# Two more slots for weight blocks in a decoder kernel, kept in mixer tiles that idle during the feed-forward blocks

## The chip, the cores and the metric

The kernel runs on one core of one Trainium2 chip. The core has a matrix engine (PE, with a queue of its own for weight loads, PEld), a vector engine (DVE), a scalar engine (ACT), a general engine (POOL) and a queue engine that issues transfers (SP). They run side by side and wait for each other by semaphores; each takes its instructions in order. The metric is device time in microseconds (us) for one execution of the whole program; the time of a kernel is the median of its runs.

## What is computed

Two layers of a decoder trunk on 256 tokens of width 1024, in float32. Each layer is a feed-forward block, a mixer and a second feed-forward block:

```python
h = x + 0.5 * (silu(n1(x) @ w_gate) * (n1(x) @ w_up)) @ w_down      # d_ff 2816
u = n(h);  P = u @ w_in                                             # one projection
h = h + concat(A(P), B(P), C(P)) @ w_out
y = h + 0.5 * (silu(n2(h) @ w_gate2) * (n2(h) @ w_up2)) @ w_down2
```

A is sparse attention with an indexer that chooses 64 keys per query (4 heads, one key head), B is attention over blocks of 256 (4 heads; with 256 tokens each query sees its own block alone), C is attention with forget gates (8 heads). A and B use rotary positions. All weights, about 195 MB with both layers, come from the chip's memory once per execution.

## The kernel before, in words

**Split products.** Every float32 weight block of 128 x 2048 (1 MB) is split into a high part `wh` (ACT, a cast, line 168) and a low part `wl` (DVE, a subtraction, line 172). PE multiplies high by high, high by low and low by high (`threes`, line 512; the matmul itself is line 366). There are four pairs of split buffers.

**Seven products instead of eight.** A feed-forward block works through 2816 columns in six units (`UNITS`, line 54). A unit of 512 columns has the weight quarters B11 and B21 (of w_gate, upper and lower half of the rows) and B12 and B22 (of w_up). The units marked "S" (1, 3 and 4) take seven products P1 to P7 of sums of quarters, after Strassen. For these, B12's tile is loaded from w_up, and then a second transfer, issued on POOL with addition (line 131, the "accumulate" below), adds B11 to it. P5 uses that sum. P6, P7 and P4 use sums that DVE forms in place (line 299, `pre`). P1, P2 and P3 use B11, B21 and B22 as they are.

**Slots.** `Weights` keeps a list of all weight blocks in the order of use (`raws`) and loads them in this order on SP (line 139). A load needs one of six tiles, the slots (`raw0` to `raw5`, 8 KB in each partition). A slot becomes free when its last reader has run, nearly always the subtraction of line 172, sometimes a `pre` of line 299. `issue` (line 110) is called at each release, and stops at the first block that finds no slot. From the first block of w_in on, the sixth slot is held back for two tiles of the mixer (`hold`, line 114), and given back at the end of the mixer's projections (`release_hold`, line 1216).

**Order of work.** The order of all products is written out by hand (`ffn_order`, line 59), and so is the mixer's (`at_step`). PE, ACT and DVE run their instructions in the order in which the program records them. `W.pump` puts a cast and a subtraction between the other instructions after each product; it looks two blocks ahead.

**The places that matter here.** Unit 1 of a block ends with P4 in PSUM bank A. Its Silu (ACT, line 653) reads that bank. Before the Silu, ACT's order has the cast of unit 3's P5 block (line 168) and the split of a transposed tile (line 680). After some transposes (line 676), PE's next product is P1 of unit 3, which starts bank A anew. In the mixer, C's queries and keys are kept in `cqa` and `cka`, all values in `va`, and A's mask in `amask`; these had tiles of their own for the whole program, and only the mixer uses them. C's queries and keys are transposed on PE in four steps (`c_T`, line 1247).

Of the kernel before, what the change touches and what calls it, by code (L numbers as in the profile page):

```python
# [18 lines left out]
P = 128  # L19
# [10 lines left out]
IDX_SCALE = (8 ** -0.5) * (64 ** -0.5)  # L30
RSQRT_MAGIC = 1597463007.0 - (1 << 22) - (1 << 30)

SLOTS = 6
SPLIT_BUFS = 4
LEAD = 2
OUT_TAIL = 3
# [37 lines left out]
class Weights:  # L74


    def __init__(self, tc, base, split_pool):
        self.nc = tc.nc
        self.base, self.split_pool = base, split_pool
        self.raws, self.pieces = [], []  # L80
        self.left = []
        self.raw_tiles, self.slot = {}, {}
        self.free = list(range(SLOTS))
        self.hold = False
        self.split_tiles, self.srcs = {}, {}
        self.n_dma = self.n_pre = self.n_high = self.n_low = self.n_used = self.n_done = 0
        self.held, self.adds = [], []
# [22 lines left out]
    def issue(self, limit=None):  # L110
        while self.n_dma < min(len(self.raws), limit or len(self.raws)):
            shape, parts, stage, more = self.raws[self.n_dma]
            if stage == "in":
                self.hold = True
            ok = [x for x in self.free if x < SLOTS - 1 or not self.hold]
            if not ok:
                return
            self.free.remove(ok[0])
            n = shape[0] * shape[1]
            t = self.base.tile([P, 2048], F32, name="raw", tag=f"raw{ok[0]}")  # L120
            self.slot[self.n_dma] = ok[0]
            self.raw_tiles[self.n_dma] = t[:, :n].rearrange("p (a b) -> p a b", a=shape[0])
            for i in range(len(parts)):
                self.load(self.n_dma, i)
            if more is not None:
                self.adds.append((self.raw_tiles[self.n_dma], more))
            self.n_dma += 1
# [2 lines left out]
        while self.adds:  # L130
            self.nc.gpsimd.dma_start(*self.adds.pop(0), accum_op=ALU.add)  # L131

    def release_hold(self):
        self.hold = False
        self.issue()

    def load(self, raw, i):
# [60 lines left out]
def kernel(ctx: ExitStack, tc: tile.TileContext, x, ffn1_norm, ffn1_w_gate, ffn1_w_up, ffn1_w_down,  # L198
# [63 lines left out]
    def add_ffn(wg, wu, wd):  # L262
        gsrc, usrc, dsrc = (w.rearrange("(k p) c -> p k c", p=P) for w in (wg, wu, wd))
        blocks, whole = {}, {}

        def block(i, kind):
            if (i, kind) not in blocks:
                _, f0, nf = UNITS[i]
                cols = slice(f0 * P, (f0 + nf) * P)
                if UNITS[i][0] == "H":  # L270
                    ks = slice(0, 4) if kind == "H0" else slice(4, 8)
                    parts = [(np.s_[:, :, 0:256], gsrc[:, ks, cols]), (np.s_[:, :, 256:512], usrc[:, ks, cols])]
                else:
                    src = gsrc if kind in ("B11", "B21") else usrc
                    k0 = 4 if kind in ("B21", "B22") else 0
                    parts = [(np.s_[:], src[:, k0:k0 + 4, cols])]
                more = gsrc[:, 0:4, cols] if UNITS[i][0] == "S" and kind == "B12" else None
                blocks[i, kind] = W.add_raw((4, 512), parts, "ffn", more)
            return blocks[i, kind]

        def raw(i, kind):
            return W.raw_tiles[blocks[i, kind]]

        def plain(i, kind, op=None):
            whole[i, op] = W.add_piece(lambda: raw(i, kind), [block(i, kind)], 2048, 4)

        def summed(i, op):
            if op == "P5":
                rids = [blocks[i, "B12"]]
                whole[i, op] = W.add_piece(lambda: raw(i, "B12"), rids, 2048, 4)  # L290
                return
            p, q, home, sign, prior = dict(P6=("B22", "B12", "B12", ALU.add, "P5"),
                                           P7=("B12", "B11", "B11", ALU.subtract, "P1"),
                                           P4=("B21", "B12", "B21", ALU.add, "P2"))[op]
            for r in (p, q):
                block(i, r)

            def pre():
                V.tensor_tensor(raw(i, home), raw(i, p), raw(i, q), op=sign)  # L299

            whole[i, op] = W.add_piece(lambda: raw(i, home), [block(i, home)], 2048, 4, pre,
                                       [blocks[i, r] for r in (p, q)], whole[i, prior])

        def down(f):
            r = W.add_raw((2, D), [(np.s_[:], dsrc[:, f:f + 2, :])], "ffn")
            W.add_piece(lambda: W.raw_tiles[r], [r], 2048, 2)

        for what in ffn_order():
            if what[0] == "G":
                if what[3] == 0:  # L310
                    plain(what[1], what[2])
            elif what[0] == "P":
                if what[2] in ("P1", "P2", "P3"):
                    if what[2] == "P1":
                        block(what[1], "B12")
                    plain(what[1], dict(P1="B11", P2="B21", P3="B22")[what[2]], what[2])
                else:
                    summed(what[1], what[2])
            elif what[0] == "d" and what[1] % 2 == 0:
                down(what[1])  # L320
        for f in TAIL[::2]:
            down(f)
# [31 lines left out]
    cs = cst[:, 384:640].rearrange("p (t c) -> p t c", t=2)  # L354
    causal = cp.tile([P, 3 * P], F32, name="causal")
    identr = cp.tile([P, P], F32R, name="identr")
    cqa = [at.tile([P, 8, 66], F32, name=f"cqa{t}", tag=f"cqa{t}") for t in range(2)]
    cka = [at.tile([P, 8, 66], F32, name=f"cka{t}", tag=f"cka{t}") for t in range(2)]
    va = [at.tile([P, 13, 65], F32, name=f"va{t}", tag=f"va{t}") for t in range(2)]
    for t in range(2):  # L360
        G.memset(cqa[t][:, :, 65:66], 1.0)
        G.memset(cka[t][:, :, 64:65], 1.0)
        G.memset(va[t][:, :, 64:65], 1.0)

    def mm(o, l, r, start, stop):
        T.matmul(o, l, r, start=start, stop=stop, skip_group_check=True)  # L366

# [381 lines left out]
    def mixer(l, entry, nxt):  # L749
# [83 lines left out]
            mm(o, q, k[1], False, stop)  # L833

        st = {}
        swapped = base.tile([P, 2, 512], F32, name="swapped", tag="sg")
        turns = itertools.count()

        def post_iq(ps):
            rot = base.tile([P, 2, 2, S], F32, name="iqr", tag="ov0")  # L840
            rot = [[rot[:, t, jj] for jj in range(2)] for t in range(2)]
            for t in range(2):
                for jj in range(2):
                    evac(rot[t][jj], ps[t][:, jj * S:(jj + 1) * S], t)
                    rope(heads(rot[t][jj], 4), cs[:, t, 0:64], cs[:, t, 64:128], V)
            qs = {}

            def split(jj):
                qs[jj] = [stack(rot[t][jj]) for t in range(2)]

            def turn_iq(jj):
                if jj == 0:
                    st["iqT"] = base.tile([P, 2, 4, S], F32R, name="iqT", tag=f"raw{SLOTS - 1}")
                queries_T(st["iqT"][:, jj], qs[jj])

            for jj in range(2):
                at_step(7 + jj, lambda jj=jj: split(jj))
                at_step(9 + jj, lambda jj=jj: turn_iq(jj))

        def post_ib(ps):  # L860
# [85 lines left out]
                                    imm_value=-3e38)  # L946

            def amask():
                am = at.tile([P, 3 * P], F32, name="amask", tag="amask")
                V.tensor_scalar(am[:, P:2 * P], st["score"][1][:, 0:P], -2e38, None, op0=ALU.is_gt)  # L950
                for t in range(2):
                    V.scalar_tensor_tensor(am[:, 2 * t * P:(2 * t + 1) * P], st["score"][t][:, t * P:(t + 1) * P],
                                           -2e38, future, op0=ALU.is_gt, op1=ALU.max)
                V.tensor_scalar(am, am, NEG, None, op0=ALU.mult)
                st["amask"] = am
# [53 lines left out]
        def post_b(ps):  # L1009
# [17 lines left out]
                    bk.append(twice.rearrange("p h s d -> p h (s d)"))  # L1027

            def bk_turn():
                st["bkT"] = base.tile([P, 2, 4, S], F32R, name="bkT", tag=f"raw{SLOTS - 1}")  # L1030
                keys_T(st["bkT"], bk)

            bk = []
# [179 lines left out]
        while side:  # L1213
            step[0] += 1
            run_side()
        W.release_hold()

        acc = [bank("acc") for _ in range(4)]

# [45 lines left out]
        for i in range(n + 1):  # L1265
            if i < n:
                scores(i)
            if i == n - 1:
                nxt = nxt()
            if i > 0:  # L1270
                flip(i - 1)
            if i < n:
                exps(i)
            if i in (3, 5, 7, 9):
                c_T((i - 3) // 2)
            if i not in (3, 5, 9, n):
                next(halves)
            if 0 < i < n:
                values(i - 1)
                if i > 2 and i % 2:  # L1280
                    outT((i - 3) // 2)
        for _ in halves:
            raise AssertionError
        return tail(acc, lhs, taken, OUT_ORDER[8 - OUT_TAIL:], 1.0, nxt,
                    (lambda: values(n - 1), lambda: outT(n // 2 - 1), lambda: None))


    def before_mixer(l):
# [73 lines left out]
```

## Time and profile before

| what | us |
|---|---|
| median of 3 runs | 1052.88 (1050.73 to 1057.02) |
| the profiled execution | 1049.79 |
| its span, first to last instruction | 1048.0 |
| PE busy | 1023.8 (98%) |
| DVE busy | 819.6 (78%) |
| ACT busy | 602.5 (57%) |
| POOL busy | 167.7 (16%) |
| bytes moved, and rate over the span | 196.74 MB, 188 GB/s |

A row of the timeline has the start in us, the duration, the engine, the line, the operation, output and inputs, and in brackets how long the engine stood before it and who ended that. Successive equal instructions stand in one row (x8) with the time from the first start to the last end. "SPq" rows are issues of transfers, not the transfers. A row of waits has who waited for whom, the total in us, how often, and the longest. A row of stretches has, for each engine, the busy time and the number of instructions, then the granted PE clock (1.00 is full), the busy share of the DMA engines and GB/s.

### The profile page before, as it was taken

How to read it: one execution, taken by the hardware profiler on the slowest of the kernel's cores; microseconds unless marked ns; L12 is line 12 of the kernel's file. 1: busy time of each engine (PE TensorE's matmuls, PEld its weight loads, DVE VectorE, ACT ScalarE, POOL GpSimd, SP SyncE). 2: the span in 40 equal slices, each digit the busy share in tenths (PEclk: the TensorE clock that was granted, in tenths of full speed). 3: DMA queues.
4: the chain of work that ended last, by engine and by line, in shares of the span. 5: the costliest groups of instructions: out<-in, count | busy, mean ns of one | idle time of the engine just before them, and what ended most of it. 6: DMA issues, size and time to landing. Idle time of an engine off the chain costs nothing. (4 is left out here: it accounts for less than half of the span.)

```text
span 1048.0 us, 12900 instructions
## 1 busy us (share of the span) xinstructions
PE 1023.8 (98%) x4982; PEld 857.2 (82%) x4982; DVE 819.6 (78%) x990; ACT 602.5 (57%) x687; POOL 167.7 (16%) x187
## 2 busy tenths in 40 slices
PE   9998999999999999999999999999999999999998
PEld 7887888897888788788878878888978878878887
DVE  5787969778777688786967878797797767779785
ACT  6554656478554656545664655556766546646461
POOL 1000040167610000000000000402766000000000
PEclk9999999999999999999999999999999999999999
DMA  9855866545362437493963749393445426284931
GB/s 351 255 168 174 282 193 246 164 167 164 139 220 92 114 137 229 163 296 115 351 194 118 247 155 302 109 327 121 166 163 168 165 88 199 82 280 136 306 121 41
DMA packets 94418, 196.74 MB, mean 188 GB/s; under 512 B 7314, under 2 KB 19986, under 8 KB 94356
## 3 DMA queue, kind: packets, MB, share of 16 engines
q1 hardware_dynamic: 87152, 180.64, 49.6%
q0 software_dynamic: 6336, 12.58, 6.6%
q10 hardware_dynamic: 868, 2.69, 0.7%
q8 instruction: 39, 0.64, 0.2%
q14 instruction: 23, 0.19, 0.1%
HBM read 194.85 MB, written 1.05 MB: 187 GB/s over the span
## 5 line engine op out<-in xcount | busy, mean ns | idle before, releaser
L172 DVE TENSOR_TENSOR wl<-raw,wh 128x2048 fp32r<-128x2048 f32 (+2 forms) x208 | 470.0, 2277 | 103.5 <-ACT wh L168 101.3
L168 ACT CAST wh<-raw 128x2048 fp32r<-128x2048 f32 (+2 forms) x208 | 389.8, 1892 | 124.3 <-PE ps_acc L366 46.1
L366 PE MATMUL ps_acc<-wh,hT 128*128 128x512 f32 (+1 forms) x704 | 185.9, 389 | 0.0
L366 PEld LDWEIGHTS ps_acc<-wh,hT 128*128 128x128 f32 x704 | 131.2, 188 | 26.8
L366 PE MATMUL ps_gu<-wh,x 128*128 128x512 f32 (+2 forms) x512 | 124.0, 385 | 0.0
L366 PE MATMUL ps_acc<-wl,hT 128*128 128x512 f32 (+1 forms) x352 | 105.9, 388 | 0.0
L366 PEld LDWEIGHTS ps_gu<-wh,x 128*128 128x128 f32 x512 | 92.8, 192 | 14.1
L131 POOL DMA_DIRECT2D raw<-in_ffn_w_gate_dram x12 | 15.9, 1322 | 490.6 <-DMA raw<-in_ffn_w_up_dram 275.4
L299 DVE TENSOR_TENSOR raw<-raw 128x2048 f32<-128x2048 f32 x36 | 82.4, 2288 | 0.1
L366 PEld LDWEIGHTS ps_acc<-wl,hT 128*128 128x128 f32 x352 | 65.9, 188 | 13.6
L366 PE MATMUL ps_A<-wh,A 128*128 128x512 f32 x256 | 65.6, 398 | 8.9 <-ACT tmp L653 8.9
L366 PE MATMUL ps_C<-wh,A 128*128 128x512 f32 x256 | 65.4, 395 | 0.1
L366 PE MATMUL ps_gu<-wl,x 128*128 128x512 f32 (+2 forms) x256 | 64.6, 374 | 0.0
L366 PE MATMUL ps_B<-wh,A 128*128 128x512 f32 x256 | 63.7, 391 | 0.0
L366 PEld LDWEIGHTS ps_A<-wh,A 128*128 128x128 f32 x256 | 46.6, 188 | 18.8 <-ACT tmp L653 9.9
L366 PEld LDWEIGHTS ps_C<-wh,A 128*128 128x128 f32 x256 | 47.6, 189 | 10.1 <-issue 0.4
L366 PEld LDWEIGHTS ps_B<-wh,A 128*128 128x128 f32 x256 | 47.8, 188 | 9.8
L366 PEld LDWEIGHTS ps_gu<-wl,x 128*128 128x128 f32 x256 | 46.9, 188 | 7.9
L366 PE MATMUL ps_A<-wh,S 128*128 128x512 f32 x192 | 47.9, 391 | 0.0
L366 PEld LDWEIGHTS ps_A<-wh,S 128*128 128x128 f32 x192 | 35.7, 188 | 7.3
L377 POOL TENSOR_TENSOR y_n<-msq,minus_half 128x1 f32<-128x1 f32 (+1 forms) x10 | 6.4, 638 | 219.5 <-DVE msq L376 219.5
L366 PE MATMUL ps_T<-wh,A 128*128 128x512 f32 x160 | 39.5, 389 | 0.0
(251 smaller groups left out, 1500.0 us busy)
## 6 DMA issues: line engine op xcount, KB each, us to landing
raw<-in_ffn_w_down_dram SPq DMA_DIRECT2D x44, 1024.0 KB, 7.4
raw<-in_ffn_w_gate_dram SPq DMA_DIRECT2D x40, 1024.0 KB, 7.0
raw<-in_ffn_w_up_dram SPq DMA_DIRECT2D x40, 1024.0 KB, 5.6
raw<-in_w_in_dram SPq DMA_DIRECT2D x24, 1024.0 KB, 5.7
raw<-in_ffn_w_gate_dram POOLq DMA_DIRECT2D x12, 1024.0 KB, 14.9
raw<-in_w_out_dram SPq DMA_DIRECT2D x8, 1024.0 KB, 4.8
raw<-in_ffn_w_gate_dram SPq DMA_DIRECT2D x8, 512.0 KB, 3.9
raw<-in_ffn_w_up_dram SPq DMA_DIRECT2D x8, 512.0 KB, 5.0
```

What stands on the lines that cost most here:

```text
L131: self.nc.gpsimd.dma_start(*self.adds.pop(0), accum_op=ALU.add)
L168: self.nc.scalar.copy(hv, src)
L172: self.nc.vector.tensor_tensor(lv, self.srcs.pop(self.n_low), hv.bitcast(F32), op=ALU.subtract)
L299: V.tensor_tensor(raw(i, home), raw(i, p), raw(i, q), op=sign)
L366: T.matmul(o, l, r, start=start, stop=stop, skip_group_check=True)
L377: G.tensor_tensor(y, dst, minus_half[:, :n], op=ALU.pow)
```

## The change

Two slots are added, `raw6` and `raw7`. The tiles behind them are those of the mixer: `cqa` and `cka` of both token halves become one tile `cqk` in `raw6`, and `va` with `amask` becomes one tile `vam` in `raw7`. In place of the flag `hold` there is a number `top`, the first slot that is not to be used: five from the first w_in block on, six after the mixer's projections, seven after the last `c_T`, eight when the last values have been multiplied. The ones in the tiles' extra columns are set at the start of each mixer, no longer once at the start of the program. And in the units of seven products, B11 stands ahead of B12 in the list of loads.

```diff
-SLOTS = 6
+SLOTS, HELD = 8, 5
+WIDTHS = {6: 4 * 8 * 66, 7: 2 * 13 * 65 + 3 * P}
@@ Weights.issue
             if stage == "in":
-                self.hold = True
-            ok = [x for x in self.free if x < SLOTS - 1 or not self.hold]
+                self.top = HELD
+            ok = [x for x in self.free if x < self.top]
...
-            t = self.base.tile([P, 2048], F32, name="raw", tag=f"raw{ok[0]}")
+            t = self.base.tile([P, WIDTHS.get(ok[0], 2048)], F32, name="raw", tag=f"raw{ok[0]}")
...
-    def release_hold(self):
-        self.hold = False
+    def open(self, top):
+        self.top = top
         self.issue()
@@ add_ffn
                 if what[2] in ("P1", "P2", "P3"):
+                    plain(what[1], dict(P1="B11", P2="B21", P3="B22")[what[2]], what[2])
                     if what[2] == "P1":
                         block(what[1], "B12")
-                    plain(what[1], dict(P1="B11", P2="B21", P3="B22")[what[2]], what[2])
@@ start of the program
-    cqa = [at.tile([P, 8, 66], F32, name=f"cqa{t}", tag=f"cqa{t}") for t in range(2)]
-    cka = [at.tile([P, 8, 66], F32, name=f"cka{t}", tag=f"cka{t}") for t in range(2)]
-    va = [at.tile([P, 13, 65], F32, name=f"va{t}", tag=f"va{t}") for t in range(2)]
-    for t in range(2):
-        G.memset(cqa[t][:, :, 65:66], 1.0)
-        G.memset(cka[t][:, :, 64:65], 1.0)
-        G.memset(va[t][:, :, 64:65], 1.0)
@@ mixer
+        qk = base.tile([P, 4, 8, 66], F32, name="cqk", tag="raw6")
+        cqa, cka = [qk[:, t] for t in range(2)], [qk[:, 2 + t] for t in range(2)]
+        vm = base.tile([P, WIDTHS[7]], F32, name="vam", tag="raw7")
+        va = [vm[:, 845 * t:845 * t + 845].rearrange("p (h d) -> p h d", h=13) for t in range(2)]
+        G.memset(qk[:, 0:2, :, 65:66], 1.0)
+        G.memset(qk[:, 2:4, :, 64:65], 1.0)
+        for t in range(2):
+            G.memset(va[t][:, :, 64:65], 1.0)
...
-                am = at.tile([P, 3 * P], F32, name="amask", tag="amask")
+                am = vm[:, 1690:]
...
-        W.release_hold()
+        W.open(HELD + 1)
...
                 c_T((i - 3) // 2)
+                if i == 9:
+                    W.open(7)
...
-                    (lambda: values(n - 1), lambda: outT(n // 2 - 1), lambda: None))
+                    (lambda: values(n - 1), lambda: (outT(n // 2 - 1), W.open(SLOTS)), lambda: None))
```

PE, ACT and DVE run the same instructions in the same order before and after. What moves is on SP and POOL. On SP, in the first feed-forward block, from the loads that end the first round of slots to unit 3's; before, `raw_106` is B12 of unit 1, `raw_170` its B11, `raw_484` B22 of unit 2, `raw_538` B12 of unit 3 and `raw_572` its B11:

```order
L139 DMA raw_106<-in_ffn1_w_up_dram 128x4x512
L346 DMA cst_78<-in_const_dram 128x512
L347 DMA fb_93<-in_forget_bias_dram 128x16
L139 DMA raw_170<-in_ffn1_w_gate_dram 128x4x512
L139 DMA raw_222<-in_ffn1_w_gate_dram 128x4x512
L139 DMA raw_263<-in_ffn1_w_gate_dram 128x4x512
L139 DMA raw_266<-in_ffn1_w_down_dram 128x2x1024
L139 DMA raw_285<-in_ffn1_w_down_dram 128x2x1024
L139 DMA raw_337<-in_ffn1_w_up_dram 128x4x512
L139 DMA raw_418<-in_ffn1_w_up_dram 128x4x512
L139 DMA raw_484<-in_ffn1_w_up_dram 128x4x512
L139 DMA raw_538<-in_ffn1_w_up_dram 128x4x512
L139 DMA raw_572<-in_ffn1_w_gate_dram 128x4x512
```

The same stretch with the change, where `raw_106` is B11 of unit 1, `raw_108` its B12, `raw_329` B22 of unit 2, `raw_410` B11 of unit 3 and `raw_476` its B12:

```order
L140 DMA raw_106<-in_ffn1_w_gate_dram 128x4x512
L140 DMA raw_108<-in_ffn1_w_up_dram 128x4x512
L140 DMA raw_110<-in_ffn1_w_gate_dram 128x4x512
L347 DMA cst_78<-in_const_dram 128x512
L348 DMA fb_93<-in_forget_bias_dram 128x16
L140 DMA raw_162<-in_ffn1_w_gate_dram 128x4x512
L140 DMA raw_214<-in_ffn1_w_down_dram 128x2x1024
L140 DMA raw_255<-in_ffn1_w_down_dram 128x2x1024
L140 DMA raw_258<-in_ffn1_w_up_dram 128x4x512
L140 DMA raw_277<-in_ffn1_w_up_dram 128x4x512
L140 DMA raw_329<-in_ffn1_w_up_dram 128x4x512
L140 DMA raw_410<-in_ffn1_w_gate_dram 128x4x512
L140 DMA raw_476<-in_ffn1_w_up_dram 128x4x512
```

Two more loads stand ahead of the constants, and each unit's B11 is ahead of its B12; counted from the first, unit 3's B12 is the 15th weight load before and the 16th now.

On POOL, at the start of a mixer, between the mixer's norm and the first rope, before:

```order
L377 TENSOR_TENSOR y_n_1492<-msq,minus_half 128x2
L770 TENSOR_TENSOR swapped<-iqr,cst 128x4x32
L771 TENSOR_TENSOR swapped<-iqr,cst 128x4x32
L770 TENSOR_TENSOR swapped<-iqr,cst 128x4x32
L771 TENSOR_TENSOR swapped<-iqr,cst 128x4x32
```

and with the change:

```order
L370 TENSOR_TENSOR y_n_1480<-msq,minus_half 128x2
L833 MEMSET cqk 128x16
L834 MEMSET cqk 128x16
L836 MEMSET vam 128x13 x2
L763 TENSOR_TENSOR swapped<-iqr,cst 128x4x32
L764 TENSOR_TENSOR swapped<-iqr,cst 128x4x32
```

Four memsets stand there that were six at the start of the program; the three accumulates of a block stay where they were in POOL's order.

More of the change, by code (lines that the diff above doesn't have):

```diff
@@ L83, in __init__ @@
         self.free = list(range(SLOTS))
-        self.hold = False
+        self.top = SLOTS
         self.split_tiles, self.srcs = {}, {}
@@ L131, in add @@
             self.nc.gpsimd.dma_start(*self.adds.pop(0), accum_op=ALU.add)
-    def release_hold(self):
-        self.hold = False
+    def open(self, top):
+        self.top = top
         self.issue()
@@ L852, in turn_iq @@
                 if jj == 0:
-                    st["iqT"] = base.tile([P, 2, 4, S], F32R, name="iqT", tag=f"raw{SLOTS - 1}")
+                    st["iqT"] = base.tile([P, 2, 4, S], F32R, name="iqT", tag=f"raw{HELD}")
                 queries_T(st["iqT"][:, jj], qs[jj])
@@ L1029, in bk_turn @@
             def bk_turn():
-                st["bkT"] = base.tile([P, 2, 4, S], F32R, name="bkT", tag=f"raw{SLOTS - 1}")
+                st["bkT"] = base.tile([P, 2, 4, S], F32R, name="bkT", tag=f"raw{HELD}")
                 keys_T(st["bkT"], bk)
```

## The prediction

> **What bounds the kernel now.** I read the page's first part, then the waits of PE, then the timeline at the longest of them, then who waits for the transfer behind it.
>
> ```profile
> PE 1023.8 (98%) x4982; PEld 857.2 (82%) x4982; DVE 819.6 (78%) x990; ACT 602.5 (57%) x687; POOL 167.7 (16%) x187
> ```
>
> PE is busy 1023.8 of 1048.0 us, so about 24 us of idle PE is all that any better arrival of data can win, as long as PE's own instructions stay as they are. The largest of PE's waits by releaser (total, times, longest; the third row is PE's weight-load queue, the last is ACT's):
>
> ```profile
> PE ps_A L366 <- ACT tmp L653: 8.9, 4, 2.9
> PE ps_acc L366 <- DVE bkT L829: 5.2, 2, 2.6
> PEld ps_A L366 <- ACT tmp L653: 9.9, 4, 3.1
> ACT wh L168 <- DMA raw<-in_ffn_w_gate_dram: 35.9, 8, 8.4
> ```
>
> The largest item is one place that occurs four times, once in each feed-forward block: PE wants bank A for P1 of unit 3, and ACT has not yet run the Silu (L653) that empties it. The second, in the mixer, waits for a computed tile and has no load behind it. The rest of PE's idle time lies in start-up and in shorter waits. This is the place in the first block:
>
> ```profile
> 80.88 1.91 ACT L168 CAST wh<-raw 128x2048 fp32r<-128x2048 f32 x1 [0.76 <-PE ps_A L366]
> 89.32 1.07 PE L366 MATMUL ps_A<-wl,A 128*128 128x512 f32 x4
> 90.23 0.60 PE L676 MATMUL ps_C<-cst,tmp 128*128 128x128 f32 x4
> 90.67 0.60 PE L676 MATMUL ps_B<-cst,tmp 128*128 128x128 f32 x4
> 91.20 1.90 ACT L168 CAST wh<-raw 128x2048 fp32r<-128x2048 f32 x1 [8.40 <-DMA raw<-in_ffn_w_gate_dram]
> 93.00 0.58 ACT L680 CAST hT<-ps_T 128x512 fp32r<-128x512 f32 x1
> 93.48 0.60 ACT L653 ACTIVATE tmp<-ps_A 128x512 f32<-128x512 f32 x1
> 94.13 2.11 PE L366 MATMUL ps_A<-wh,A 128*128 128x512 f32 x8 [2.86 <-ACT tmp L653]
> ```
>
> ACT is in order. It stands 8.40 us before the cast of unit 3's P5 block, whose accumulate transfer (B12 + B11, issued on POOL) has not landed; behind that cast are queued the split of hT and the Silu, and PE waits for the Silu. The two groups of four transposes start 0.44 us apart, so PE would have gone on at 90.67 + 0.44 = 91.11 instead of 94.13: 3.02 us lost. The other three places, by the last transposes and the late matmul:
>
> ```profile
> 425.42 0.60 PE L676 MATMUL ps_B<-cst,tmp 128*128 128x128 f32 x4
> 428.31 0.98 PE L366 MATMUL ps_A<-wh,A 128*128 128x512 f32 x3 [2.29 <-ACT tmp L653]
> 607.49 0.60 PE L676 MATMUL ps_B<-cst,tmp 128*128 128x128 f32 x4
> 609.84 1.43 PE L366 MATMUL ps_A<-wh,A 128*128 128x512 f32 x5 [1.76 <-ACT tmp L653]
> 940.95 0.60 PE L676 MATMUL ps_B<-cst,tmp 128*128 128x128 f32 x4
> 943.59 1.65 PE L366 MATMUL ps_A<-wh,A 128*128 128x512 f32 x6 [2.03 <-ACT tmp L653]
> ```
>
> They lose 2.45, 1.91 and 2.20 us, and the four together 9.58 us. All of it hangs on four of the twelve accumulates (line L131: who waited for it, and its issue to landing):
>
> ```profile
>   ACT wh L168: 31.1, 4
> DMA to landing us min/median/max: 8.7/14.9/16.5
> ```
>
> **The change part by part.** *PE, ACT and DVE* keep their instructions and their order, so what can move is when loads land.
>
> *Two more slots and the swapped order.* When does unit 3's B12 start? Loads leave SP in order, each when a slot is free. In the first block its load is the 15th before; six need no release, so it waits for the ninth freed block. Afterwards it is the 16th, because B11 goes first; eight need no release, so it waits for the eighth. The eighth release is the one on which the load ahead of it, unit 2's B22, left before. One row per block shows both loads (two issues of 0.37 us, start of the first, then the distance to the end of the second):
>
> ```profile
> 58.42 10.16 SPq L139 DMA_DIRECT2D raw<-in_ffn_w_up_dram  x2
> 393.18 10.16 SPq L139 DMA_DIRECT2D raw<-in_ffn_w_up_dram  x2
> 575.23 10.16 SPq L139 DMA_DIRECT2D raw<-in_ffn_w_up_dram  x2
> 908.69 10.16 SPq L139 DMA_DIRECT2D raw<-in_ffn_w_up_dram  x2
> 74.57 1.31 POOL L131 DMA_DIRECT2D raw<-in_ffn_w_gate_dram  x1 [50.38 <-DMA raw<-in_ffn_w_up_dram]
> ```
>
> So the load starts 10.16 - 0.37 = 9.79 us earlier in all four blocks, at 58.42 instead of 68.21. It took 74.57 - 68.21 = 6.36 us to the accumulate's start. With the same flight the accumulate starts at 64.8, and with the slowest accumulate of the trace (16.5) it lands at 81.3. ACT ends its previous cast at 80.88 + 1.91 = 82.79: ACT's DMA wait is gone. The latest landing that costs PE nothing: the Silu's input is complete at 89.32 + 1.07 = 90.39, and a cast and a split (91.20 to 93.48, 2.28 us) must be through by then, so 90.39 - 2.28 = 88.1. The margin is 6.8 us with the slowest accumulate and 14.6 with the fastest.
>
> What is late next? The Silu cannot start before 90.39; with 0.60 us it ends at 91.0, and PE is ready at 91.11. Bounds for what is left: nothing, or one whole Silu, 0.6 us at each place (2.4). I take 0.1 in all, since the chain closes by itself. **Gain: 9.5 us**, ends 7.2 and 9.6.
>
> *Loads that are no longer waited for elsewhere.* ACT's other 35.9 - 31.1 = 4.8 us on these transfers lie in start-up, where PE shows no wait for that cast; I count nothing. If that cover failed, B12 of unit 1 would be the one to watch: it goes out seventh instead of sixth.
>
> ```profile
> 22.73 1.46 POOL L131 DMA_DIRECT2D raw<-in_ffn_w_gate_dram  x1 [8.47 <-DMA raw<-in_ffn_w_up_dram]
> 49.64 1.90 ACT L168 CAST wh<-raw 128x2048 fp32r<-128x2048 f32 x1
> 352.30 1.38 POOL L131 DMA_DIRECT2D raw<-in_ffn_w_gate_dram  x1 [0.17 <-issue]
> ```
>
> One more 1 MB load ahead of it costs a flight of 6.36 us at most, so its accumulate lands at 22.73 + 6.36 + 16.5 = 45.6 at worst, and its cast is at 49.64. In the second block it also goes out one load later, but its accumulate is held until 352.30 by work on POOL, not by the load. SP's small loads behind the added ones (constants, head gains) are first used in the mixer.
>
> *Memsets moved.* Six short ones leave the start; four stand ahead of the mixer's first rope on POOL.
>
> ```profile
> 1.00 0.12 POOL L363 MEMSET va<- 128x13 f32 x1
> 198.14 0.72 POOL L377 TENSOR_TENSOR y_n<-msq,minus_half 128x2 f32<-128x2 f32 x1 [41.02 <-DVE msq L376]
> 203.16 1.37 POOL L770 TENSOR_TENSOR swapped<-iqr,cst 128x128 f32<-128x128 f32 x1 [4.30 <-ACT iqr L797]
> ```
>
> Four at 0.12 are 0.5 us in POOL's 4.30 us of waiting for ACT: nothing. Their slots' last readers are casts of the block before, over by then. If that cover were gone, the rope would be 0.5 us later.
>
> *Sum.* The profiled execution took 1049.79 us (span 1048.0). 1049.79 - 9.5 = 1040.3. The median of the three runs, 1052.88, lies 3.1 above that execution, so **1043.4 us** as a median.
>
> **Is the accumulate as fast when more loads are queued?** Stretches of 6 us around it (last columns: granted clock, DMA share, GB/s):
>
> ```profile
> 62.00:68.00 6.00, 6.00 (x29) 4.95 (x28) 6.00 (x3) 3.79 (x4) 0.00 (x0) 1.00 0.15 58
> 74.00:80.00 6.00, 6.00 (x28) 4.95 (x27) 5.56 (x4) 3.71 (x2) 1.31 (x1) 1.00 1.03 339
> 80.00:86.00 6.00, 6.00 (x28) 4.98 (x27) 5.23 (x6) 2.03 (x2) 0.00 (x0) 1.00 1.07 299
> ```
>
> The loads that SP issues in that time, beside the one of 68.21:
>
> ```profile
> 70.42 2.57 SPq L139 DMA_DIRECT2D raw<-in_ffn_w_gate_dram  x2
> 74.82 2.57 SPq L139 DMA_DIRECT2D raw<-in_ffn_w_down_dram  x2
> 79.75 0.37 SPq L139 DMA_DIRECT2D raw<-in_ffn_w_up_dram  x1
> ```
>
> The accumulate now runs in full DMA engines (339 GB/s, 299 GB/s); afterwards it starts where they are nearly idle (share 0.15), and six loads, released at the same instants, join it from 68 on. [...]
>
> **The rivals.**
> 1. *Partly late.* The longer queue of loads slows the accumulate until it lands between 88.1 and 91.2 in the first block. It would need 23.3 to 26.4 us where the slowest took 16.5. Half of the gain: 1048.
> 2. *Slower: the accumulate falls behind the six loads.* Decided by a landing after 91.2. Six loads of 1.05 MB at 339 GB/s take 18.6 us from 68.2, to 86.8; the fastest accumulate (8.7) after them ends at 95.5, 4.3 us later than now. Four places: 1052.9 + 17 = 1070. Against it: it already runs beside loads in full engines and took 16.5.
> 3. *The clock.* Each mixer has a stretch at half clock right after PE's wait for bkT:
>
> ```profile
> 255.90:259.40 3.50, 3.13 (x9) 2.65 (x10) 2.87 (x7) 1.56 (x3) 1.86 (x6) 0.56 0.76 282
> 771.60:775.10 3.50, 3.13 (x9) 2.65 (x10) 2.89 (x7) 1.58 (x3) 1.85 (x6) 0.51 0.70 282
> ```
>
> At 0.56 and 0.51 they cost 1.5 and 1.7 us. The mixers now come 3.0 and 7.4 us earlier. If what lowers the clock keeps its own time base, these stretches may vanish (1043.4 - 3.3 = 1040) or each double (1047). [...]
> 4. *The change doesn't do what it says:* PE waits at the same place for something else as long as before, for instance because ACT's cast needs a wh buffer that PE frees late. ACT's casts before it wait only 0.76 us for PE. Time unchanged, 1053.
>
> **How the numbers follow.** Forecast 0.77, rival 1 0.06, rival 2 0.04, rival 3 0.08 (half each way), rival 4 0.05. The forecast's own range, from its ends 7.2 and 9.6 and some 2.5 us for a median of few runs, is 1040.5 to 1048; rival 3 takes the low end down, rivals 1 and 4 push up: 1038.5 to 1050. A measurement here tells about 0.5%, 5.3 us, from no change. Faster by more: nearly all of the forecast, most of rival 3 and some of rival 1, 0.84; within: the rest of these and rival 4, 0.12; slower: rival 2, 0.04.
>
> **What would show it.** Right: in the changed profile PE's wait for the Silu is under 1 us in all; ACT has no wait for a gate transfer outside start-up; unit 3's accumulate starts near 65 in the first block and some 10 us earlier, against PE's work, in the others; and PE's busy time stays near 1024. Wrong: the wait stays with an earlier accumulate (rival 4), the accumulate takes over 20 us (1 and 2), or the mixers' clock changes (3).

## The result

| kernel | median, us | lowest to highest | runs |
|---|---|---|---|
| before, beside it | 1053.74 | 1050.73 to 1057.02 | 4 |
| changed | 1037.03 | 1035.87 to 1040.45 | 4 |

Two later executions of the kernel before, at mean clocks of 0.753 and 0.85 (1266.95 and 1130.63 us), are left out of every figure here and below.

The ratio is 0.9846, with a 95% interval of 0.9807 to 0.9886: the change wins 16.7 us, where 9.5 were forecast, and the time lies below the forecast range. The profiled execution took 1035.87 us (span 1034.1), against 1049.79 (span 1048.0) before.

The changed kernel's busy time, from the page, and the two largest of PE's waits:

```profile
PE 1018.8 (99%) x4982; PEld 854.4 (83%) x4982; DVE 820.6 (79%) x990; ACT 601.6 (58%) x687; POOL 167.8 (16%) x189
```

```profile
PE ps_acc L359 <- DVE bkT L822: 5.4, 2, 2.7
PE ps_acc L393 <- DVE tmp L413: 2.7, 2, 1.4
```

The wait for the Silu, 8.9 us before, is not in the list any more. The wait for bkT in the mixer stands as it did. PE runs the same 4982 instructions, but is busy 5.0 us less: something made the same matmuls shorter.

The place in the first block, in the changed kernel's timeline (the Silu is line 646 now, the split of hT line 673):

```profile
63.38 1.31 POOL L132 DMA_DIRECT2D raw<-in_ffn_w_gate_dram  x1 [35.13 <-DVE wl L173]
...
80.32 1.91 ACT L169 CAST wh<-raw 128x2048 fp32r<-128x2048 f32 x1 [0.77 <-PE ps_A L359]
85.76 1.91 ACT L169 CAST wh<-raw 128x2048 fp32r<-128x2048 f32 x1 [3.53 <-PE ps_B L359]
87.58 0.57 ACT L673 CAST hT<-ps_T 128x512 fp32r<-128x512 f32 x1
89.88 0.60 ACT L646 ACTIVATE tmp<-ps_A 128x512 f32<-128x512 f32 x1 [1.74 <-PE ps_A L359]
90.12 0.60 PE L669 MATMUL ps_B<-cst,tmp 128*128 128x128 f32 x4
90.53 2.11 PE L359 MATMUL ps_A<-wh,A 128*128 128x512 f32 x8
```

The accumulate starts at 63.38 (74.57 before). The cast of unit 3's P5 block runs at 85.76 and waits for PE alone, no longer for a transfer; the Silu follows its input at once, and P1 starts 0.41 us after the last transposes, without a gap. Of the accumulates' landings (8.6 to 15.8 us after the issue) nobody waits. So the step that the forecast rests on came out as worked out, and 9.6 us of the gain are told.

The second thing that changed is the clock. These are the stretches in the mixers behind PE's wait for bkT, at the same places in the program as those at a granted clock of 0.56 and 0.51 before (columns: busy time and instructions of PE, PEld, DVE, ACT and POOL, the granted clock, DMA share, GB/s):

```profile
252.40:255.90 3.50, 3.20 (x15) 2.71 (x16) 3.28 (x7) 2.04 (x3) 1.80 (x6) 1.00 0.71 276
761.50:765.00 3.50, 3.19 (x15) 2.71 (x16) 3.28 (x7) 2.03 (x3) 1.80 (x6) 1.00 0.71 280
```

They are at full clock, though the wait ahead of them is still there: the prediction priced them at 1.5 and 1.7 us. 9.6 + 3.2 = 12.8 of the 13.9 us between the two spans. The two medians are 16.7 apart, though, and the four executions of the changed kernel had mean granted clocks of 0.998, 0.998, 0.996 and 0.993 at 1035.87, 1036.02, 1038.04 and 1040.45 us. The question for the experiments is what the clock has to do with the change.

### The profile page after: what moved, and what is told of

Its sections match the earlier page's. It is cut to its first block, busy times and chain, and to the rows that moved or that the text cites. A ratio compares the mean times of both kernels' runs of the same rounds, so it can differ in the third digit from the quotient of the medians.

```text
span 1034.1 us, 12904 instructions
## 1 busy us (share of the span) xinstructions
PE 1018.8 (99%) x4982; PEld 854.4 (83%) x4982; DVE 820.6 (79%) x990; ACT 601.6 (58%) x687; POOL 167.8 (16%) x189
## 4 chain that ended last, share of the span: by engine, by line
PE 92%; DVE 5%; issue 1%; ACT 1%; DMA 1%; POOL 0%; SPq 0%; DVEq 0%; POOLq 0%
PE ps_acc L359 28%; PE ps_gu L359 16%; PE ps_A L359 15%; PE ps_B L359 13%; PE ps_C L359 8%; PE ps_T L359 7%; DVE wl L173 2%; PE ps_T L669 1%; PE ps_acc L393 1%; DVE score L926 1%; PE ps_C L669 1%; DMA raw<-in_ffn_w_gate_dram 1%; PE ps_gu L1254 1%; PE ps_gu L1133 1%; DVE tmp L1119 0%
## 5 line engine op out<-in xcount | busy, mean ns | idle before, releaser
L359 PE MATMUL ps_gu<-wh,x 128*128 128x512 f32 (+2 forms) x512 | 121.3, 379 | 0.0
L359 PE MATMUL ps_C<-wh,A 128*128 128x512 f32 x256 | 64.8, 393 | 0.1
```

## The experiments

Two explanations are weighed. **Landing alone**: the four waits for the Silu are worth 9.6 us, the rest is the chance of a few executions. **Landing and clock**: the four waits are themselves gaps that can send PE to half clock for 3.4 us (1.7 us lost each time), so that their going takes these stretches with it. A rival to both is that the added slots bring something at other places.

All ratios are against the kernel before on the same chip, with 95% intervals; the clock is the mean of the granted clocks of the timed executions.

| kernel | median, us | ratio | clock |
|---|---|---|---|
| changed, again | 1037.16 | 0.9841 (0.9820 to 0.9862) | 0.997 |
| 7 slots, old order | 1037.66 | 0.9846 (0.9823 to 0.9868) | 0.998 |
| 7 slots, new order | 1045.60 | 0.9919 (0.9892 to 0.9946) | 0.995 |
| 6 slots, new order | 1062.85 | 1.0082 (1.0053 to 1.0111) | 0.988 |
| 8 slots, old order | 1039.42 | 0.9862 (0.9830 to 0.9895) | 0.996 |
| before, without unit 3's accumulate | 1038.80 | 0.9857 (0.9837 to 0.9877) | 0.997 |
| before, waits filled with transposes | 1052.36 | 0.9978 (0.9959 to 0.9997) | 0.996 |
| changed, a third time | 1037.96 | 0.9856 (0.9829 to 0.9884) | 0.997 |
| changed, wait for bkT filled | 1037.49 | 0.9845 (0.9816 to 0.9875) | 0.998 |
| changed, part B one step later | 1032.57 | 0.9796 (0.9766 to 0.9826) | 0.998 |
| the same, on another chip | 1033.18 | 0.9803 (0.9776 to 0.9831) | 0.998 |

The kernel before ran 34 times beside these: 1054.7 us in the median, mean clock 0.9915.

### The changed kernel again

No edit.

> The changed kernel as it is, in five rounds beside the kernel before, for the granted clock of each execution. Two theories of the gain of 16.7 us in the medians. Landing alone: 9.6 us come from the four waits for the Silu, the rest is the chance of a few executions, and five rounds give a gain near 9.6 to 12. Landing and clock: the four waits are themselves gaps that sometimes put PE into a stretch of half clock (3.4 us long, about 1.7 us dearer each), so the kernel before has more such stretches per execution; then the gain stays at 14 to 18, and within each kernel the time falls as the granted clock rises, by about 10 us for each 0.01 of clock, with a lower mean clock in the kernel before.

Measured: 1037.16 against 1054.17, a gain of 17.0. It isn't the chance of a few executions. The clocks were 0.995, 0.998, 0.998 and 0.998, against 0.990 to 0.994 of the eight executions before. Within the 34 executions of the kernel before, a straight line through time and clock falls by 9.2 us for 0.01 of clock. Landing alone is out.

The profiled execution of this run (1038.80 us, clock 0.995) is not as lucky as the one above: it has half clock behind both waits for bkT.

```profile
254.13:257.54 3.41, 3.41 (x11) 2.66 (x10) 2.44 (x3) 2.43 (x3) 0.30 (x1) 0.52 0.29 117
762.72:766.13 3.41, 2.81 (x8) 2.43 (x9) 2.79 (x7) 1.31 (x4) 2.08 (x6) 0.52 0.80 308
```

The first profile of the kernel before (1049.79 us, 0.995) has these two as well, and both have one in start-up and no other before the last microseconds. With the same stretches at half clock, then, the change wins 11.0 us.

### A second profile of the kernel before

No edit.

> The kernel before once more, for a second profile of it, because the profiled execution had a granted clock of 0.995 where eight other executions had 0.990 to 0.994 (mean 0.992). Clock theory: a stretch of half clock of 3.4 us follows where some 1.9 us or more of PE's standing still fall into one of the windows of 3.4 us that run on from start to end, and the phase of these windows differs from execution to execution; so in this one, one or more of the four places where PE waits for the Silu is followed by a stretch at half clock, which the first profile had behind none of them. Rival, the clock only depends on the mixer's wait for bkT and on start-up: no stretch of half clock behind the four places.

Measured: 1055.90 us at a clock of 0.989. PE's wait for the Silu is as long as in the first profile (9.0 us against 8.9), and yet this execution is 6.1 us longer:

```profile
PE ps_A L366 <- ACT tmp L653: 9.0, 4, 3.0
```

The stretches around the four places, cut to within 0.15 us along the windows in which the clock changed (second column from the left the busy PE; third from the right the clock):

```profile
91.49:94.90 3.41, 1.01 (x4) 0.86 (x5) 2.01 (x1) 3.31 (x5) 0.00 (x0) 1.00 0.04 16
94.90:98.32 3.42, 3.42 (x10) 2.65 (x9) 3.42 (x6) 0.00 (x0) 0.00 (x0) 0.52 0.00 0
425.98:429.40 3.42, 1.45 (x11) 1.07 (x9) 0.75 (x1) 2.68 (x3) 0.00 (x0) 1.00 0.60 232
429.40:432.81 3.41, 3.15 (x8) 2.48 (x8) 3.41 (x5) 1.17 (x3) 0.00 (x0) 0.52 0.00 0
610.28:613.70 3.42, 1.61 (x9) 1.20 (x8) 2.19 (x1) 3.15 (x5) 0.00 (x0) 1.00 0.23 88
613.70:617.11 3.41, 3.41 (x10) 2.65 (x9) 3.41 (x6) 0.17 (x1) 0.00 (x0) 0.52 0.03 7
944.79:948.20 3.41, 1.41 (x11) 1.06 (x10) 1.12 (x1) 3.06 (x4) 0.00 (x0) 1.00 0.55 212
948.20:951.62 3.42, 3.42 (x9) 2.64 (x10) 3.42 (x5) 0.79 (x2) 0.00 (x0) 0.52 0.02 5
```

Behind all four places stands a stretch at half clock. The reader can see its price in the first matmuls of P1: eight of them take 2.86 us here, and took 2.11 in the execution that the prediction read.

```profile
93.89 2.86 PE L366 MATMUL ps_A<-wh,A 128*128 128x512 f32 x8 [3.01 <-ACT tmp L653]
```

In the first profile of the kernel before, the same four waits were followed by full clock. The windows of the first, second and third place, with the one behind the first and the third:

```profile
88.90:92.31 3.41, 2.37 (x15) 1.84 (x13) 0.00 (x0) 1.11 (x1) 0.00 (x0) 1.00 0.89 317
92.31:95.73 3.42, 1.60 (x7) 1.34 (x8) 2.60 (x2) 2.74 (x5) 0.00 (x0) 1.00 0.01 5
95.73:99.14 3.41, 3.41 (x17) 2.83 (x16) 3.41 (x5) 1.95 (x2) 0.00 (x0) 1.00 0.00 0
...
426.75:430.16 3.41, 1.85 (x8) 1.53 (x9) 2.86 (x3) 2.47 (x5) 0.00 (x0) 1.00 0.01 5
...
607.78:611.19 3.41, 1.65 (x9) 1.20 (x8) 2.34 (x2) 2.97 (x5) 0.00 (x0) 1.00 0.17 65
611.19:614.60 3.41, 3.41 (x17) 2.83 (x16) 3.41 (x5) 1.71 (x2) 0.00 (x0) 1.00 0.02 7
```

Here the border between two windows fell into the first wait, so that each window got a part of it (2.37 and 1.60 us of busy PE). In the second profile the wait lay 2.3 us deep in one window (1.01 us of busy PE), and the next ran at half clock. At the third place of the first profile the whole wait of 1.76 us lay in one window (1.65 us of busy PE), and full clock followed: it was just too short. The stretches of half clock in the second profile start within 0.15 us of 94.90, 429.40, 613.70 and 948.20, which are 98, 54 and 98 windows of 3.413 us apart. The 3.413 us are measured: by the clock records of the first profile the two stretches behind the waits for bkT are as long, at a granted clock of 0.50, and they start at 256.29 and 771.70, 151 such lengths apart and 72 from the one in start-up (10.53) to the first. So in both profiles the windows run on from stretch to stretch, and how they lie against PE's work differs between the two executions. In the execution that the prediction read they lay well.

### One added slot, old order

```diff
-SLOTS, HELD = 8, 5
+SLOTS, HELD = 7, 5
@@ the changed kernel's tile in raw7 and its order of loads undone
-        va, amask in the tile vam (raw7)
+        va, amask in tiles of their own, as before
-                    plain(what[1], dict(P1="B11", P2="B21", P3="B22")[what[2]], what[2])
                     if what[2] == "P1":
                         block(what[1], "B12")
+                    plain(what[1], dict(P1="B11", P2="B21", P3="B22")[what[2]], what[2])
```

> One added slot (queries and keys of C), values and mask in tiles of their own as before, B12 loaded ahead of B11 as before. Unit 3's B12 is then the 15th load with seven slots, so it waits for the eighth release, as in the changed kernel. Landing: its load starts near 58, the accumulate near 65 in the first block, the four waits for the Silu are gone, and the time is that of the changed kernel within 3 us (1034 to 1041). Rival, the second slot or the swap matters by itself (start-up, other blocks): a part of the gain is missing, 1043 or more.

The accumulate in the first block:

```profile
64.89 1.31 POOL L132 DMA_DIRECT2D raw<-in_ffn_w_gate_dram  x1 [39.56 <-DVE wl L173]
```

Measured: 1037.66, the changed kernel's time (1037.16 on the same chip). PE's waits for the Silu are gone at all four places. The load counts as the 15th on the eighth release, and that is enough: neither the eighth slot nor the new order is needed.

### One added slot, new order

The same, with the order of loads of the changed kernel.

> The same one added slot, but with B11 ahead of B12. Unit 3's B12 is then the 16th load with seven slots and waits for the ninth release, as in the kernel before. Landing: its load starts near 68, its accumulate near 74.6, the four waits for the Silu stay at 8 to 10 us in all, and the time is that of the kernel before within 3 us (1050 to 1056). Rival, one more slot helps by itself because all other loads come earlier: a gain of 4 us or more, 1048 or less.

Measured: 1045.60. The number lies in the rival's range (1048 or less), but the rows show another reason than the rival's. PE's wait for the Silu (line 650 here), and the load of B12, the accumulate and ACT's cast in the first block:

```profile
PE ps_A L363 <- ACT tmp L650: 4.4, 4, 1.2
```

```profile
67.54 0.37 SPq L140 DMA_DIRECT2D raw<-in_ffn_w_up_dram  x1
73.67 1.31 POOL L132 DMA_DIRECT2D raw<-in_ffn_w_gate_dram  x1 [45.61 <-DMA raw<-in_ffn_w_up_dram]
...
88.87 1.91 ACT L169 CAST wh<-raw 128x2048 fp32r<-128x2048 f32 x1 [6.75 <-DMA raw<-in_ffn_w_gate_dram]
```

The load leaves at the ninth release (67.54; 68.21 before), as counted. But the cast follows the accumulate's issue after 88.87 - 73.67 = 15.20 us, not after 91.20 - 74.57 = 16.63. At the four places 1.39, 1.37, 1.18 and 1.11 us are lost, from start to start, 5.05 in all: 4.5 less than before. That leaves waits of under 1.4 us, and in this execution none of them is followed by half clock; its clock of 0.995 comes from start-up and the mixers. Landing holds for the instant of the load; its assumption that an accumulate takes as long in any company does not.

### Six slots, new order

```diff
                 if what[2] in ("P1", "P2", "P3"):
+                    plain(what[1], dict(P1="B11", P2="B21", P3="B22")[what[2]], what[2])
                     if what[2] == "P1":
                         block(what[1], "B12")
-                    plain(what[1], dict(P1="B11", P2="B21", P3="B22")[what[2]], what[2])
```

> The kernel before with six slots, and only B11 loaded ahead of B12. Unit 3's B12 is the 16th load with six slots, one release later than before (near 70.3 us in the first block, 2.2 later). Landing, with accumulates as long as before: each of the four waits grows by 2.2 us, 8.8 in all, 1063 in the median, more with the clock. Landing, with accumulates that the swapped order shortens by 1.1 us, as the seven slots with the swap showed (waits of 1.1 to 1.4 us in place of 1.9 to 3.0 at the same instant of the load): each wait grows by 1.1 only, 4.4 in all, 1058. If it was the slot and not the order that shortened them: 1063 again.

PE's wait for the Silu, and the load, the accumulate and the cast in the first block:

```profile
PE ps_A L366 <- ACT tmp L653: 15.4, 4, 4.0
```

```profile
70.06 0.37 SPq L139 DMA_DIRECT2D raw<-in_ffn_w_up_dram  x1
...
77.27 1.31 POOL L131 DMA_DIRECT2D raw<-in_ffn_w_gate_dram  x1 [48.12 <-DMA raw<-in_ffn_w_up_dram]
...
91.98 1.90 ACT L168 CAST wh<-raw 128x2048 fp32r<-128x2048 f32 x1 [9.50 <-DMA raw<-in_ffn_w_gate_dram]
```

Measured: 1062.85 against 1055.24, slower by 0.8%. The load leaves at 70.06, as counted, and the cast follows the accumulate's issue after 14.71 us. So it is the order that shortens the accumulate, with six slots as with seven. The load ahead of it took longer, though (77.27 - 70.06 = 7.21 us, against 6.36), and the waits grew by 15.4 - 9.0 = 6.4 us, 1.6 each, between the two expected sizes. The median is nevertheless the 1063 that was expected with accumulates as long as before: the clock fell too, from 0.991 to 0.988, and in this profile two of the four places have two windows of half clock in place of one.

While one of unit 3's accumulates is under way, SP's queue moves 4.1 to 4.2 MB in the first profile of the kernel before and 3.3 to 3.7 MB with the new order, and both queues together move 300 to 320 GB/s in either. So fewer bytes of loads run beside it; why the order leaves fewer was not settled. The new order alone costs some 8 us, and in the change the second slot buys it back.

### Before, without unit 3's accumulate

```diff
-                more = gsrc[:, 0:4, cols] if UNITS[i][0] == "S" and kind == "B12" else None
+                more = gsrc[:, 0:4, cols] if UNITS[i][0] == "S" and kind == "B12" and i != 3 else None
```

> The kernel before, with six slots and its own order of loads; the accumulate of unit 3 is left out in all four blocks, so that P5 of unit 3 works with B12 alone instead of B12 + B11 (the addition of B11 there is the part of the computation that is missing). Landing: the cast of that block no longer waits for a transfer, the four waits of PE for the Silu vanish with no slot added, and the profile falls by 9.6. Landing and clock: the executions fall by more than that, by 14 to 17, to 1036 to 1041 in the median, and the granted clock rises to that of the changed kernel. Rival, the added slots bring the rest of the gain: the median stays at 1043 or above.

```profile
PE ps_acc L366 <- DVE bkT L829: 5.2, 2, 2.6
```

That is the first row of PE's waits; the Silu has none. Measured: 1038.80 at a clock of 0.997, 15.4 us below the kernel before, with its six slots and its order. The accumulate's late landing is the cause, and its going brings the clock with it. What the slots bring beyond that can't be told from nothing: 1.6 us lie between this and the changed kernel on the same chip, and the intervals overlap.

### Before, with PE kept busy in the four waits

```diff
-            for j in range(nf):
-                T.transpose(ps[:, j * P:(j + 1) * P], u[f"h{t}"][:, j * P:(j + 1) * P], ident)
+            for _ in range(5 if (i, t) == (2, 1) else 1):
+                for j in range(nf):
+                    T.transpose(ps[:, j * P:(j + 1) * P], u[f"h{t}"][:, j * P:(j + 1) * P], ident)
```

> The kernel before, where the four transposes that PE runs just ahead of its wait for the Silu are repeated four times (16 of 0.11 us, 1.8 us of work that changes nothing, in a gap of 1.9 to 3.0 us). Clock theory: the lost time of the four places stays (9.6 us from the last needed transpose to P1), but PE stands still for at most 1.3 us in each, so no stretch of half clock follows them; the granted clock rises from 0.992 to 0.994 to 0.996 and the median falls by 2 to 5 us, to 1049 to 1052. Rival, idle PE at these places has nothing to do with the clock: clock as before, the median within 1 us of 1054, or up to 2 us above it where the added work outlasts a wait.

The transposes and P1 in the first block:

```profile
93.96 2.35 PE L677 MATMUL ps_B<-cst,tmp 128*128 128x128 f32 x20
97.83 2.12 PE L366 MATMUL ps_A<-wh,A 128*128 128x512 f32 x8 [1.52 <-ACT tmp L653]
```

Measured: the clock rose from 0.991 to 0.996 (twelve executions, 0.993 to 0.998), and the median fell by 2.9 us, to 0.4 us above the range that was expected, with the interval at 0.4% to nearly nothing, though PE has 7 us of work more. P1 starts at full clock: eight matmuls in 2.12 us. The four places lost some 2 us more than in the second profile of the kernel before, from start to start (64 added transposes of 0.11 us, and some 1.7, 0.6, 1.3 and 1.2 us of standing still, 11.8 in all against 9.7), so the clock's share is some 5 us. This tells the clock from the landing: the waits are there, the half clock is not.

### The changed kernel with part B one step later

The longest stretch of standing still that is left behind start-up, and the one that still brings half clock in some executions, is the mixer's wait for bkT (2.7 us). The same window and the next, in another execution of the changed kernel (the third series):

```profile
250.60:254.10 3.50, 1.07 (x6) 0.99 (x7) 3.28 (x12) 1.89 (x4) 3.27 (x7) 1.00 1.00 325
254.10:257.50 3.40, 3.40 (x10) 2.61 (x9) 2.81 (x5) 2.70 (x3) 0.58 (x2) 0.52 0.42 172
```

```diff
-B_TURN, B_STEP, A_ROOT, A_TURN = 18, 20, 22, 26
+B_TURN, B_STEP, A_ROOT, A_TURN = 18, 21, 22, 26
```

> The changed kernel with the scores, exponentials and products of mixer part B one step later (3.2 us of projection work), so that the low part of bkT is ready when PE reaches the first score. If PE's wait for bkT (2.7 us, twice) is all that stands there: 5.4 us less and a granted clock of 0.998 in nearly all executions, 1030 to 1032 in the median. Rival, B's chain then ends later than the projections and PE waits at the end of the mixer for what was waited for before: 1036 or more.

The first row of PE's waits, and the first score in the timeline:

```profile
PE ps_acc L393 <- DVE tmp L413: 2.7, 2, 1.4
```

```profile
254.28 0.84 PE L359 MATMUL ps_acc<-bkT,bqT 128*128 128x128 f32 x4
```

Measured: 1032.57, clock 0.998, 0.998, 0.997 and 0.998. The wait for bkT is gone: the four matmuls of the first score run in one go, where the changed kernel had one, a wait of 2.70, and three. The time is 0.6 us above the range that was expected.

Again, beside the changed kernel on one chip:

> The changed kernel with part B's scores one step later, once more beside the changed kernel: 4 to 6 us faster than it (two waits of 2.7 us gone), 1031 to 1034, clock 0.998 or 0.997 in all executions. If the 4.6 us between the two medians on different chips were the chip's, less than 2 us.

> The changed kernel beside the three others of this series, on the same chip: 1036 to 1038 in the median, with granted clocks between 0.993 and 0.998.

Measured: 1033.18 (1031.34 to 1034.14) and 1037.96 (1037.00 to 1039.69). The two do not overlap. This version beats both kernels, by 4.8 us the changed one.

### The changed kernel with the wait for bkT filled

```diff
                 b = bank(tag)
+                if hs[i] == ("B", 0):
+                    for _ in range(14):
+                        mm(b[:, P:3 * P], q[:, P:S], k[0][:, 0:S], True, True)
```

> The changed kernel, where PE repeats a product of B's first score fourteen times (256 columns each, about 1.6 us) in the 2.7 to 2.8 us in which it waits for the low part of bkT. Clock theory: PE then stands still for some 1.2 us only, less than the 1.9 us of one window that brought the half clock in the profiles so far, so no stretch of half clock follows in the mixers: clock 0.998 in every execution, the slow executions of the changed kernel (1038 to 1040) vanish, the median falls by up to 1 us. Rival, the half clock there does not come from the standing still: clocks as scattered as in the changed kernel, same median.

Measured: clock 0.998 in all four executions, 1037.49 against 1037.96. The clock did what was expected; half a microsecond in the time can't be told from nothing.

### Eight slots, old order

The changed kernel without its new order of loads.

> Eight slots without the swapped order: unit 3's B12 is the 15th load with eight slots and waits for the seventh release, one earlier than in the changed kernel. Landing: the four waits are gone already at the eighth release, so an earlier landing buys nothing: 1036 to 1038, the same as the changed kernel within 2 us. Rival, earlier loads go on paying elsewhere: 1034 or less; or the swapped order is needed: 1040 or more.

Measured: 1039.42, clocks 0.995 to 0.998. The accumulate starts at 54.32 in the first block, and the four waits are gone. The ratio, 0.9862, is the changed kernel's on the same chip, 0.9856, within the intervals; the median is 1.4 us above the expected range. A release earlier buys nothing.

## Why the prediction was wrong in its size

**What bounds it, and the four waits: right.** The 9.58 us of lost time at the four places went whole: in every profile of the changed kernel P1 starts 0.4 us after the last transposes. Where only the accumulate was taken away, they went too.

**The instant of the load: right.** The accumulate started at 63.38, forecast 64.8; by the counting of slots and releases the six combinations of slots and order fall as they should in the instant of their loads (48, 58 to 59, 68 and 70 us). B12's flight was estimated too long, 6.36 us where it took 5.5. The accumulate landed 8.6 to 9.3 us after its issue, with only 0.3 to 0.5 MB on SP's queue beside it; nobody waits for it, and the margin was never used.

**The rest at nothing: nearly right.** One place beyond the four gains, at the start of the second layer. On POOL an accumulate and a step of the norm, on which PE's next transposes wait through DVE, stand close together. The two rows in the kernel before and in the changed kernel (run again):

```profile
525.29 1.28 POOL L131 DMA_DIRECT2D raw<-in_ffn_w_gate_dram  x1 [63.31 <-DVE trunk L535]
526.08 1.09 POOL L377 TENSOR_TENSOR y_n<-msq,minus_half 128x1 f32<-128x1 f32 x1
...
516.73 1.28 POOL L132 DMA_DIRECT2D raw<-in_ffn_w_gate_dram  x1 [65.07 <-DMA raw<-in_ffn_w_up_dram]
519.92 0.56 POOL L370 TENSOR_TENSOR y_n<-msq,minus_half 128x1 f32<-128x1 f32 x1 [1.90 <-DVE msq L369]
```

With the slots the accumulate goes out earlier, the norm's step takes 0.56 us in place of 1.09, and PE gains some 0.5 us there. Between these two executions, which have the same stretches at half clock, the 11.0 us are 9.7 at the four places, 0.5 here, 0.6 in start-up and 0.2 in all else. The 0.6 are not the change's: start-up differs by 0.4 us between the two profiles of the kernel before, and is 0.7 us longer than in the first of them with one added slot. Against the memsets no run speaks.

**What failed is the sum**, in two of its terms that are one. The first is the base: the 3.1 us by which the median of the three runs lies above the profiled execution were carried over to the changed kernel as if they belonged to any execution. The clocks of those three are not on record. The 34 executions since show what such a gap is made of: stretches at half clock, of which the profiled execution (0.995) had fewer than most (0.9915 in the mean). In the second profile the four more of them stand behind the very waits that the change removes. The second is rival 3, the clock: it looked for half clock only where the profile showed it, behind the wait for bkT, priced at 3.3 us and given 0.08. That a wait of the same length in the feed-forward block could bring the same was not drawn from it, because the profile showed four such waits without. Half clock behind the four waits is worth up to 4 x 1.7 = 6.8 us in one execution. Of the prediction's own signs, two pointed at the clock: PE's busy time fell to 1018.8 us, where it was to stay near 1024, and the mixers' clock changed.

The sum as the runs have it: (1 - 0.9915) x 1052 = 8.9 us of clock before, (1 - 0.9969) x 1036 = 3.2 after (14 executions). 9.6 for the waits and 5.7 for the clock make 15.3 of the 16.4 us by which the means of all these executions differ; 0.5 more is the start of the second layer, and where the last half microsecond lies is open.

**Rivals.** 1 and 2 (a slower accumulate) did not come: it landed faster in all four blocks. 4 is out. Rival 3 happened, not as an accident of phase in the mixers but as a part of the gain. That both stretches of the mixers vanished in the one profile after was the luck of that execution: of the two other profiles of the same kernel one has one, and one has both.

The prediction also took the two parts of the change together. They pull in opposite directions: the added slots bring the load two releases forward, the new order puts it one place back.

## What to carry to other kernels

Where short waits of a matrix engine repeat, ask how many executions the profile stands for: if the profiled one has a higher granted clock than the others (here 0.995 against 0.9915 in the mean), its waits can be dearer than it shows, by half-clock stretches behind them. In this kernel a wait of 2 to 3 us is to be priced at its length plus half of a clock window (1.7 of 3.413 us) times the chance that enough of it, some 1.9 us, falls into one window. Do not carry the gap between a profile and a median over to the changed kernel before it is known what the gap is made of. Where a change has two parts that move the same transfer, count each alone: here one slot without the new order does all that the change does.

## What was unexpected of the hardware

**Two microseconds were enough for half clock.** Take the pauses of over 1 us that the fourteen traces show before a matmul behind start-up, and cut them along the windows (those at half clock themselves left out). In 41 windows PE stood still for 1.0 to 1.87 us, and no half clock followed; in 22 it stood still for 1.81 to 2.91 us, and half clock followed each time. In these traces the bound lies where the two overlap, from 1.81 to 1.87 us, a little over half of a window of 3.413 us. In the first profile of the kernel before, the windows ahead of the two half-clock stretches in the mixers held 2.60 and 2.34 us of standing still; the one at the third of the four places held 1.76, and full clock followed. No window had to be idle as a whole: at the four places of the second profile PE was busy for 1.01 to 1.61 us of the window ahead of the half clock.

**An accumulate took longer beside more loads.** Unit 3's four accumulates land 16.0 to 16.5 us after their issue in the first profile of the kernel before, 14.6 to 15.4 with the other order of loads and six or seven slots, and 8.6 to 9.3 in the changed kernel. SP's queue moves 4.1 to 4.2, 3.3 to 3.7 and 0.3 to 0.5 MB beside them.
